# Two of four weight-block sums per seven-product unit: from VectorE to adding transfers

## The chip, the cores and the metric

One core of one Trainium2 chip runs the whole program. The metric is device time in microseconds (us), from the first to the last instruction of one execution and what lies around it; for the kernel before, the median of three timed executions is given. A separate execution was taken with the hardware profiler, and all rows below are from that one.

## The reference

One inference step of a two-layer decoder trunk in float32, for 512 prompt tokens and 8 x 8 sample tokens (576 columns in all), model width 1024:

```
x = x + 0.5 * ffn(x);  x = x + mixer(rmsnorm(x));  x = x + 0.5 * ffn(x)      # twice: S5 mixer, then gated-convolution mixer
ffn(x) = (silu(h @ Wgate) * (h @ Wup)) @ Wdown,  h = rmsnorm(x),  Wgate, Wup: 1024 x 4096,  Wdown: 4096 x 1024
```

At the end stand a final norm and the new states. The four FFN halves and the convolution mixer (whose input projection is 1024 x 3072) hold nearly all of the multiplications.

## The kernel before, in words

Each float32 product is made of three TensorE products on split operands: an operand is written as a high part (`h`, made by ScalarE's copy, ACT in the rows) and the remainder (`l`, made by VectorE's subtraction, DVE in the rows), and h·h, l·h and h·l are summed in PSUM. So every weight block has to be loaded, split by ACT and then by DVE before TensorE (PE) may use it.

The first FFN half, the S5 mixer and the first part of its output projection run in a fixed order. From line 1610 on (`later`), the rest runs from a list made by a planner: `late_glu`, `late_ffn(0, 1)`, `late_ffn(1, 0)`, `late_conv`, `late_ffn(1, 1)`. In this part the gate, up and convolution-input projections use a seven-product scheme (`class Seven`, line 1049): a unit of 1024 x 256 weights, one 1 MB transfer, is cut in four blocks, and with four sums of weight blocks and the matching sums of activations seven block products of 12 matmuls each (84 in all, 288 columns each) take the place of eight. There are 108 such units: 32 in each of the three FFN halves and 12 in the convolution. In an FFN half a group of four units is followed by a group of four "down" steps (192 matmuls, two 1 MB transfers, the plain three-product scheme of `Step` and `step_ops`).

`Seven.weights` (lines 1059 to 1084) prepares one unit from its loaded tile `raw` (seen as `v`, block (h, a) being `v[:, :, h, a]`):

- line 1066, `s1`: `st[1] = v(0,1) + v(1,1)`, on DVE;
- line 1070, `s3`: `v(0,1) = v(0,1) + v(0,0)` in place, on DVE, after `s1`, since it overwrites what `s1` reads;
- line 1080: `st[0] = st[1] + v(0,0)`, on DVE; line 1074, `s4`: `s4f = st[0] + v(1,0)`, on DVE;
- three splits of 128 x 1024 into `wh` (line 1044, ACT) and `wl` (line 1047, DVE): `r1` from `v(0,·)` after `s3`, `s12` from `st` after line 1080, `r2` from `v(1,·)` after the load; and a split of 128 x 512 (`s4h`, `s4l`) after `s4`.

What sets the order: `in_order` (line 938) replays a list of operations with modelled costs. Loads (SP queue), PE and GpSimd operations (POOL in the rows) keep the order in which they were created; for DVE and ACT the planner picks, among those that can begin first, the one with the earliest due time (`late`). The instruction streams come out in this order and each engine then runs its stream strictly in order, waiting on semaphores. Buffers are part of the plan: two `raw` tiles (a unit's tile is free when `r1`, `r2` and `s4` are done, and only then does the SP queue load the unit after the next into it), four pairs `wh`/`wl` (taken in the order r1, s12, r2 of unit after unit), two `st` tiles, two `s4f` tiles, four PSUM tiles.

Between two stages (an FFN half and the next one, or the convolution) DVE has other work that PE waits for: the residual additions (line 1346), the sums of squares (line 1236), the sums and remainders of the new activations (`tk`, lines 1175 to 1191), the norm (lines 1253 to 1264). Within the convolution it also has the gates and the three taps (lines 1487 to 1491). The seven products are evacuated by ACT (lines 1142, 1145, 1147, 1154) and DVE (1148, 1151, 1156).

Of the kernel before, what the change touches and what calls it, by code (L numbers as in the profile page):

```python
# [13 lines left out]
MUL, ADD, SUB = ALU.mult, ALU.add, ALU.subtract  # L14

P = 128
# [9 lines left out]
G = 64  # L26
# [7 lines left out]
def trunk_kernel(ctx: ExitStack, tc: tile.TileContext, a, o):  # L34
    nc = tc.nc
    V, S, T, GP, SP = nc.vector, nc.scalar, nc.tensor, nc.gpsimd, nc.sync
# [64 lines left out]
    class Unit:  # L101
        def __init__(self, src, nk, w):
            self.src, self.nk, self.w, self.left = src, nk, w, w * nk // D
# [807 lines left out]
            self.pool, self.n, self.t = pool, n, 0.0  # L911

    class Op:
        def __init__(self, eng, cost, fn, deps=(), take=(), give=(), due=12.0):
            self.eng, self.cost, self.fn, self.give = eng, cost, fn, give
            self.deps = [d for d in deps if d is not None]
            self.take, self.users, self.end = take, [], None
            self.left = len(self.deps)
            for d in self.deps:
                d.users.append(self)  # L920
            if eng == "PE":
                self.late = clock[0]
                clock[0] += cost
            else:
                self.late = clock[0] + due
            for p in take:
                fifo.setdefault(p, []).append(self)
            ops.append(self)
# [3 lines left out]
    def dve(n, fn, deps=(), **kw):  # L932
        return Op("V", 0.12 + 1.085e-3 * n, fn, deps, **kw)
# [4 lines left out]
    def in_order():  # L938
        for o in reversed(ops):
            for d in o.deps:  # L940
                d.late = min(d.late, o.late - d.cost)
        now = {e: 0.0 for e in ("PE", "V", "S", "SP", "G", "J")}
        queue = {e: [o for o in ops if o.eng == e] for e in ("PE", "SP", "G")}
        at = {e: 0 for e in queue}
        ready = {e: [o for o in ops if o.eng == e and not o.left] for e in ("V", "S", "J")}
        count = len(ops)

        def begin(o, t):
            for d in o.deps:
                t = max(t, d.end + 0.15)  # L950
            need = {}
            for p in o.take:
                need[p] = need.get(p, 0) + 1
            for p, n in need.items():
                if any(f is not o for f in fifo[p][:n]) or len(free[p]) < n:
                    return None
                t = max(t, sorted(free[p])[n - 1] + 0.15)
            return t

        while count:  # L960
            best = None
            for e, t in now.items():
                if e in queue:
                    c = queue[e][at[e]:at[e] + 1]
                    c = [o for o in c if not o.left]
                else:
                    c = ready[e]
                c = [(b, o) for b, o in ((begin(o, t), o) for o in c) if b is not None]
                if c:
                    first = min(b for b, _ in c)  # L970
                    b, o = min(((b, o) for b, o in c if b <= first + 0.1), key=lambda bo: bo[1].late)
                    if best is None or b < best[0]:
                        best = (b, o)
            assert best, [(e, queue[e][at[e]].fn) for e in queue if at[e] < len(queue[e])]
            b, o = best
            for p in o.take:
                fifo[p].remove(o)
                free[p].remove(min(free[p]))
            o.end = b + o.cost
            if o.eng != "J":  # L980
                o.fn()
                now[o.eng] = o.end
            if o.eng in queue:
                at[o.eng] += 1
            else:
                ready[o.eng].remove(o)
            for h in o.give:
                h.n -= 1
                h.t = max(h.t, o.end)
                if h.n == 0:  # L990
                    free[h.pool].append(h.t)
            for u in o.users:
                u.left -= 1
                if not u.left and u.eng in ready:
                    ready[u.eng].append(u)
            count -= 1
        return now
# [11 lines left out]
    def late_tile(pool, tag, shape, dt, name):  # L1009
        return B[pool].tile(list(shape), dt, name=nm(name), tag=tag)  # L1010
# [21 lines left out]
    def load_op(u):  # L1032

        if not hasattr(u, "load_op"):
            u.hold = Hold("raw", u.left)
            u.load_op = Op("SP", 5.0, u.load, take=["raw"])
        return u.load_op

    def split_ops(box, src, n, tags, deps, pool="w", give=()):

        def hi():
            p = B["s4"] if pool == "s4" else wp
            box["h"], box["l"] = (p.tile([P, 4, n, P], F32R, name=nm(t), tag=t) for t in tags)
            S.activation(box["h"], src(), AF.Copy)  # L1044

        h = scal(512 * n, hi, deps, take=[pool])
        return dve(512 * n, lambda: V.tensor_sub(box["l"], src(), raw32(box["h"])), [h], give=give)  # L1047

    class Seven:
# [9 lines left out]
        def weights(self):  # L1059
            u = self.unit  # L1060
            ld = load_op(u)

            def s1():
                v = self.v()
                self.st = late_tile("st", "st", [P, 4, 2, P], F32, "st")
                V.tensor_add(self.st[:, :, 1], v[:, :, 0, 1], v[:, :, 1, 1])

            def s3():
                v = self.v()
                V.tensor_add(v[:, :, 0, 1], v[:, :, 0, 1], v[:, :, 0, 0])  # L1070

            def s4():
                self.s4f = late_tile("s4f", "s4f", [P, 4, 1, P], F32, "s4f")
                V.tensor_add(self.s4f[:, :, 0], self.st[:, :, 0], self.v()[:, :, 1, 0])

            st = Hold("st", 2)
            a = dve(512, s1, [ld], take=["st"])
            b = dve(512, s3, [a])
            self.k_r1 = split_ops(self.r1, lambda: self.v()[:, :, 0], 2, ("wh", "wl"), [b], give=[u.hold])
            c = dve(512, lambda: V.tensor_add(self.st[:, :, 0], self.st[:, :, 1], self.v()[:, :, 0, 0]), [a])  # L1080
            self.k_s12 = split_ops(self.s12, lambda: self.st, 2, ("wh", "wl"), [c], give=[st])
            d = dve(512, s4, [c], take=["s4f"], give=[st, u.hold])
            self.k_r2 = split_ops(self.r2, lambda: self.v()[:, :, 1], 2, ("wh", "wl"), [ld], give=[u.hold])
            self.k_s4 = split_ops(self.s4, lambda: self.s4f, 1, ("s4h", "s4l"), [d], pool="s4", give=[Hold("s4f", 1)])
# [831 lines left out]
```

## Time and profile before

| What | Value |
|---|---|
| Three timed executions | 2775.16, 2779.84, 2782.81 us (median 2779.84) |
| Profiled execution, its time | 2784.35 us |
| Profiled execution, its span | 2782.6 us |
| PE, DVE, ACT, POOL busy share | 98%, 72%, 41%, 5% |
| Mean granted TensorE clock | 0.985 |
| DMA traffic | 285.07 MB, mean 102 GB/s |

The profiled execution lies 4.5 us (0.16%) above the median of the timed ones, and its own time 1.75 us above its span. PE's busy time comes from pipelined matmuls with modelled ends, so the count of matmuls in a stretch tells more than the share.

### The profile page before, as it was taken

What the parts mean: (1) busy time and instruction counts of PE and PEld (TensorE: products, weight loads), DVE (VectorE), ACT (ScalarE), POOL (GpSimd) and SP (SyncE); (2) the same over time, 40 slices, a digit from 0 to 9 for tenths busy, and PEclk for the clock granted to TensorE, in tenths of its full rate; (3) what the DMA queues carried; (4) which work ended last, traced back from release to release, by engine and by line L of the source; (5) the groups of instructions that cost most, each with busy time, mean ns of one, the idle gap of its engine ahead of it and who ended that gap; (6) DMA issues with size and microseconds to landing.
All of it is one profiled execution on the core that took longest, in us unless ns stands there. A gap on an engine that the chain in (4) does not pass through costs nothing.

```text
span 2782.6 us, 47469 instructions
## 1 busy us (share of the span) xinstructions
PE 2716.7 (98%) x20398; PEld 2691.4 (97%) x20398; DVE 2005.1 (72%) x2719; ACT 1148.6 (41%) x1638; POOL 134.7 (5%) x213
## 2 busy tenths in 40 slices
PE   8999999999999999999999999999899999999997
PEld 8999999998999999999989999999899999999997
DVE  5767655547558777777797777777898877777775
ACT  4222243423335444444464444434545544444444
POOL 3010122202200000000000000000000000000000
PEclk9999999998899999999999999999999999999999
DMA  6256444537322223332222332322222222333231
GB/s 134 87 157 167 136 132 131 155 121 248 117 81 77 91 92 91 92 92 92 92 62 92 92 92 92 92 91 92 66 87 92 77 91 92 92 92 92 91 92 50
DMA packets 227267, 285.07 MB, mean 102 GB/s; under 512 B 17460, under 2 KB 179616, under 8 KB 227024
## 3 DMA queue, kind: packets, MB, share of 16 engines
q1 hardware_dynamic: 217504, 256.86, 30.6%
q0 software_dynamic: 9376, 24.98, 3.0%
q8 instruction: 160, 2.62, 0.4%
q10 hardware_dynamic: 176, 0.20, 0.1%
q14 instruction: 51, 0.42, 0.0%
HBM read 260.19 MB, written 21.80 MB: 101 GB/s over the span
## 4 chain that ended last, share of the span: by engine, by line
PE 91%; DVE 6%; DMA 1%; ACT 1%; issue 1%; POOL 0%; POOLq 0%; DVEq 0%; ACTq 0%
PE ps L138 48%; PE ps L1110 40%; PE ps L1654 1%; DVE wl L1047 1%; DVE tk L1191 1%; PE ps L777 0%; DMA raw<-in_ffn_w_gate_up_dram 0%; PE ps L776 0%; DVE acc L1236 0%; PE ps L603 0%; DMA prow<-in_conv_w_dram 0%; DVE scr L764 0%; DVE g L756 0%; PE ps L1677 0%; DVE scr L765 0%
## 5 line engine op out<-in xcount | busy, mean ns | idle before, releaser
L1110 PE MATMUL ps<-tk,wh 128*128 128x288 f32 x5184 | 1061.3, 297 | 7.5 <-DVE tk L1191 2.9
L1110 PEld LDWEIGHTS ps<-tk,wh 128*128 128x128 f32 x5184 | 843.3, 189 | 11.3 <-DVE tk L1191 4.0
L1110 PE MATMUL ps<-tk,wl 128*128 128x288 f32 x2592 | 767.4, 296 | 8.3 <-DVE wl L1047 8.3
L138 PE MATMUL ps<-h,wh 128*128 128x288 f32 x3968 | 694.4, 295 | 0.1
L138 PEld LDWEIGHTS ps<-h,wh 128*128 128x128 f32 x3968 | 584.5, 188 | 1.9 <-DVE x L227 1.3
L1110 PEld LDWEIGHTS ps<-tk,wl 128*128 128x128 f32 x2592 | 490.2, 189 | 10.5 <-DVE wl L1047 10.0
L138 PE MATMUL ps<-h,wl 128*128 128x288 f32 x1984 | 424.0, 295 | 0.0
L138 PE MATMUL ps<-xg,wh 128*128 128x288 f32 x2048 | 362.9, 298 | 1.9 <-DVE xg L1850 1.9
L1044 ACT ACTIVATE wh<-raw 128x1024 fp32r<-128x1024 f32 x216 | 227.5, 1053 | 240.8 <-PE ps L138 231.3
L138 PEld LDWEIGHTS ps<-h,wl 128*128 128x128 f32 x1984 | 319.6, 188 | 0.0
L1047 DVE TENSOR_TENSOR wl<-raw,wh 128x1024 fp32r<-128x1024 f32 x216 | 263.6, 1220 | 67.5 <-ACT wh L1044 67.4
L138 PEld LDWEIGHTS ps<-xg,wh 128*128 128x128 f32 x2048 | 304.1, 190 | 4.5 <-DVE xg L1850 2.2
L1346 DVE SCALAR_TENSOR_TENSOR x<-ps,x 128x576 f32<-128x576 f32 x184 | 139.1, 757 | 130.1 <-PE ps L138 128.1
L138 PE MATMUL ps<-xg,wl 128*128 128x288 f32 x1024 | 220.0, 297 | 0.0
L1110 PE MATMUL ps<-tk,s4h 128*128 128x288 f32 x864 | 193.0, 299 | 10.4 <-DVE c L1148 7.4
L1044 ACT ACTIVATE wh<-st 128x1024 fp32r<-128x1024 f32 x108 | 114.5, 1060 | 196.6 <-PE ps L138 115.7
L127 DVE TENSOR_TENSOR wl<-raw,wh 128x1024 fp32r<-128x1024 f32 x103 | 126.7, 1231 | 85.4 <-ACT wh L126 85.2
L1322 ACT ACTIVATE wh<-raw 128x1024 fp32r<-128x1024 f32 x113 | 119.4, 1056 | 151.1 <-PE ps L138 121.1
L1325 DVE TENSOR_TENSOR wl<-raw,wh 128x1024 fp32r<-128x1024 f32 x113 | 137.8, 1220 | 46.7 <-ACT wh L1322 46.6
L138 PEld LDWEIGHTS ps<-xg,wl 128*128 128x128 f32 x1024 | 165.9, 190 | 0.0
L126 ACT ACTIVATE wh<-raw 128x1024 fp32r<-128x1024 f32 x103 | 108.4, 1053 | 126.1 <-PE ps L138 76.2
L1110 PEld LDWEIGHTS ps<-tk,s4h 128*128 128x128 f32 x864 | 146.1, 190 | 13.1 <-issue 7.0
(367 smaller groups left out, 3187.8 us busy)
## 6 DMA issues: line engine op xcount, KB each, us to landing
raw<-in_ffn_w_gate_up_dram SPq DMA_DIRECT2D x126, 1024.0 KB, 5.9
raw<-in_ffn_w_down_dram SPq DMA_DIRECT2D x64, 1024.0 KB, 5.1
raw<-in_conv_w_in_dram SPq DMA_DIRECT2D x12, 1024.0 KB, 5.1
raw<-in_ssm_w_glu_dram SPq DMA_DIRECT2D x8, 1024.0 KB, 5.3
pri<-pw_d SPq DMA_DIRECT2D x16, 256.0 KB, 9.3
bri<-bb_d SPq DMA_DIRECT2D x16, 256.0 KB, 8.5
ws_d<-ws POOLq DMA_DIRECT2D x8, 512.0 KB, 4.8
wy_d<-wy POOLq DMA_DIRECT2D x8, 512.0 KB, 2.9
```

The source lines that it names most:

```text
L126: S.activation(self.wh, src, AF.Copy)
L127: V.tensor_sub(self.wl, src, raw32(self.wh))
L138: T.matmul(self.ps[m][:, b, :NH], wt[:, k, c], x[:, part, b * NH:(b + 1) * NH], start=k == 0 and wt is self.wh and part == 0, stop=k == se ...
L1044: S.activation(box["h"], src(), AF.Copy)
L1047: return dve(512 * n, lambda: V.tensor_sub(box["l"], src(), raw32(box["h"])), [h], give=give)
L1110: T.matmul(ps, wt[:, k, sel], box[k][:, part, slot], start=term in ("Q1", "Q2", "S3") and k == 0 and wt is w["h"] and part == 0, stop=k == ...
L1191: V.tensor_sub(got[j][:, 1, a:b], s, raw32(got[j][:, 0, a:b]))
L1322: S.activation(st.wh, u.v[:, :, st.sub * w:(st.sub + 1) * w], AF.Copy)
L1325: st.ready = dve(D, lambda: V.tensor_sub(st.wl, u.v[:, :, st.sub * w:(st.sub + 1) * w], raw32(st.wh)), [h], give=[u.hold])
L1346: stt(h2(x[:, i]), ps()[:, :, :NH], scale, h2(x[:, i]), op0=MUL, op1=ADD)
L1654: T.matmul(pst[i][:, 0, :NH], wt[:, k, m * P:(m + 1) * P], hs[k][:, part, cols], start=k == 0 and wt is st.wh and part == 0, stop=k == 3 a ...
```

## The change

In `weights`, the sums of lines 1066 and 1070 no longer run on VectorE. For `st[1]`, the SP queue copies block (0,1) from the weights in DRAM into `st` once more, and a transfer issued by GpSimd then adds block (1,1) from DRAM onto it. For `v(0,1)`, a transfer issued by GpSimd adds block (0,0) from DRAM onto the loaded tile. So each unit has three more transfers of 256 KB, one on the SP queue and two on GpSimd's. The sums of lines 1080 and 1074 stay on VectorE. The planner's operations get a `lag`: time until the result can be used, in which the queue is already free.

```
     class Op:
-        def __init__(self, eng, cost, fn, deps=(), take=(), give=(), due=12.0):
+        def __init__(self, eng, cost, fn, deps=(), take=(), give=(), due=12.0, lag=0.0):
...
-                d.late = min(d.late, o.late - d.cost)
+                d.late = min(d.late, o.late - d.cost - d.lag)
...
-            o.end = b + o.cost
+            o.end = b + o.cost + o.lag
...
-                now[o.eng] = o.end
+                now[o.eng] = b + o.cost
...
-            u.load_op = Op("SP", 5.0, u.load, take=["raw"])
+            u.load_op = Op("SP", 4.5, u.load, take=["raw"], lag=1.0)
...
-            def s1():
-                v = self.v()
+            def block(h, m):
+                return u.src.rearrange("(k h p) (m c) -> p k h m c", h=2, p=P, m=2)[:, :, h, m]
+
+            def a21():
                 self.st = late_tile("st", "st", [P, 4, 2, P], F32, "st")
-                V.tensor_add(self.st[:, :, 1], v[:, :, 0, 1], v[:, :, 1, 1])
-
-            def s3():
-                v = self.v()
-                V.tensor_add(v[:, :, 0, 1], v[:, :, 0, 1], v[:, :, 0, 0])
+                SP.dma_start(self.st[:, :, 1], block(0, 1))
...
-            a = dve(512, s1, [ld], take=["st"])
-            b = dve(512, s3, [a])
+            b = Op("G", 0.7, lambda: GP.dma_start(self.v()[:, :, 0, 1], block(0, 0), accum_op=ADD), [ld], lag=4.0)
+            a = Op("SP", 1.3, a21, take=["st"], lag=2.0)
+            a = Op("G", 0.7, lambda: GP.dma_start(self.st[:, :, 1], block(1, 1), accum_op=ADD), [a], lag=4.0)
```

The split `r1` now depends on `b` (the adding transfer onto `v(0,1)`), and line 1080's sum depends on the second `a` (the adding transfer onto `st`).

## Rows read from the trace of the kernel before

**Rows 1.** Page: busy time of the engines; then shares of the chain of waits.

```profile
PE 2716.7 (98%) x20398; PEld 2691.4 (97%) x20398; DVE 2005.1 (72%) x2719; ACT 1148.6 (41%) x1638; POOL 134.7 (5%) x213
PE 91%; DVE 6%; DMA 1%; ACT 1%; issue 1%; POOL 0%; POOLq 0%; DVEq 0%; ACTq 0%
```

**Rows 2.** Busy by stretch: length, PE, PEld, DVE, ACT, POOL (x count), PEclk, DMA share, GB/s.

```profile
831.00:864.00 33.00, 28.30 (x184) 26.23 (x183) 26.38 (x36) 18.73 (x28) 0.00 (x0) 0.95 0.13 36
864.00:1372.00 508.00, 508.00 (x3827) 507.96 (x3825) 377.62 (x463) 215.04 (x295) 0.00 (x0) 1.00 0.30 92
...
1402.00:1440.00 38.00, 31.07 (x198) 29.50 (x198) 34.29 (x47) 20.87 (x30) 1.04 (x2) 0.91 0.22 63
...
1979.00:2040.00 61.00, 53.88 (x360) 51.75 (x359) 54.20 (x73) 29.86 (x51) 0.00 (x0) 0.92 0.22 70
2040.00:2150.00 110.00, 104.48 (x765) 102.67 (x764) 100.42 (x138) 52.46 (x99) 0.00 (x0) 0.98 0.29 94
...
2188.00:2218.00 30.00, 26.57 (x187) 24.98 (x186) 24.99 (x34) 17.94 (x26) 0.00 (x0) 1.00 0.18 55
```

**Rows 3.** Groups by line and shape: the two sums in question, whole run.

```profile
L1066 DVE TENSOR_TENSOR st<-raw 128x512 f32<-128x512 f32 x108 | 74.5, 689 | 76.7 <-DMA raw<-in_ffn_w_gate_up_dram 76.2
L1070 DVE TENSOR_TENSOR raw<-raw 128x512 f32<-128x512 f32 x108 | 73.8, 683 | 0.1
```

**Rows 4.** Timeline of VectorE and TensorE: start, length, line, count, [idle before <- releaser].

```profile
832.13 0.69 DVE L1066 TENSOR_TENSOR st<-raw 128x512 f32<-128x512 f32 x1
839.72 0.53 PE L1110 MATMUL ps<-tk,wh 128*128 128x288 f32 x2 [1.12 <-DVE tk L1191]
...
851.03 0.69 DVE L1066 TENSOR_TENSOR st<-raw 128x512 f32<-128x512 f32 x1 [0.40 <-DMA raw<-in_ffn_w_gate_up_dram]
855.02 0.61 PE L1110 MATMUL ps<-tk,s4l 128*128 128x288 f32 x1 [1.28 <-DVE s4l L1047]
...
1407.76 0.42 PE L1110 MATMUL ps<-tk,wl 128*128 128x288 f32 x1 [2.33 <-DVE wl L1047]
1430.38 0.37 PE L1110 MATMUL ps<-tk,s4h 128*128 128x288 f32 x1 [3.29 <-DVE c L1148]
...
2069.28 0.40 PE L1110 MATMUL ps<-tk,wl 128*128 128x288 f32 x1 [1.10 <-DVE wl L1047]
2104.98 0.40 PE L1110 MATMUL ps<-tk,wl 128*128 128x288 f32 x1 [1.78 <-DVE wl L1047]
```

**Rows 5.** Chain of waits in order of time: start, us, what.

```profile
1209.68 44.53 PE ps L1110 x336
...
1405.97 0.60 DVE raw L1070
...
2064.38 0.53 DVE raw L1070
...
2101.05 0.60 DVE raw L1070
```

**Rows 6.** Timeline of SP, VectorE and ScalarE: a unit within an FFN, then one in the convolution.

```profile
1223.84 0.37 SPq L111 DMA_DIRECT2D raw<-in_ffn_w_gate_up_dram  x1
1229.85 0.69 DVE L1066 TENSOR_TENSOR st<-raw 128x512 f32<-128x512 f32 x1 [0.26 <-DMA raw<-in_ffn_w_gate_up_dram]
1235.47 1.05 ACT L1044 ACTIVATE wh<-raw 128x1024 fp32r<-128x1024 f32 x1
...
2084.03 0.69 DVE L1066 TENSOR_TENSOR st<-raw 128x512 f32<-128x512 f32 x1
2087.41 1.05 ACT L1044 ACTIVATE wh<-raw 128x1024 fp32r<-128x1024 f32 x1
```

**Rows 7.** Transfers issued by GpSimd: issue time (ns min/median/max); then KB each, us to landing.

```profile
L444 POOL DMA_DIRECT2D b_in<-in_ssm_b_re_dram x1: 1729/1729/1729, 39.3 to 39.3; - x1
...
b_in<-in_ssm_b_re_dram POOLq DMA_DIRECT2D x1, 256.0 KB, 6.2
y<-y_d POOLq DMA_DIRECT2D x8, 288.0 KB, 3.5
```

More of the change, by code (lines that the diff above doesn't have):

```diff
@@ L913, in trunk_kernel @@
     class Op:
-        def __init__(self, eng, cost, fn, deps=(), take=(), give=(), due=12.0):
-            self.eng, self.cost, self.fn, self.give = eng, cost, fn, give
+        def __init__(self, eng, cost, fn, deps=(), take=(), give=(), due=12.0, lag=0.0):
+            self.eng, self.cost, self.fn, self.give, self.lag = eng, cost, fn, give, lag
             self.deps = [d for d in deps if d is not None]
```

## Prediction

> **What bounds the kernel now.** I read the page's busy shares first: PE is busy 98%, DVE 72%, POOL 5% [rows 1]. As PE's ends are modelled, the busy share alone doesn't say that PE is the limit, so I turned to the chain of waits, 91% of which is PE and 6% DVE [rows 1]: the change takes work from an engine that holds a sixteenth of the chain. Then the busy time by stretch. From 864 to 1372 us, an FFN half in the planned part, PE issues 3827 matmuls in 508.00 us with no gap: 0.1327 us each, at the full granted clock [rows 2]. DVE is idle a quarter of that time. No relief of DVE can shorten such a stretch, and the other two planned FFN halves repeat it. Against that pace the stretches between the stages lose time: length less count x 0.1327 gives 8.6 us in 831 to 864, 11.7 in 1402 to 1440, 13.2 in 1979 to 2040, 8.5 in 2040 to 2150 (the convolution) and 5.2 in 2188 to 2218 [rows 2], 47 us in all. There DVE is busy 80 to 91% of the time, and twice PE's granted clock falls to a mean of 0.91 or 0.92. These 47 us are the ceiling of what the change can give. The timeline then shows which DVE instruction ends PE's waits there [rows 4], and the chain of waits whether a removed sum stands in front of it [rows 5].
>
> **What it removes.** Two of DVE's sums in each of 108 units: 74.5 + 73.8 = 148 us of DVE's 2005 [rows 1, 3]. In the FFN halves that is worth nothing (PE covers it; if PE were quicker, it would come to count). Stage by stage, against the profiled execution:
>
> - GLU to FFN, 831 to 864. The sum of line 1066 at 832.13 stands in DVE's stream ahead of the `tk` for which PE waits 1.12 us at 839.72: 0.6 us (its 0.69, less the overlap of neighbours that the chain shows as pieces of 0.60 [rows 5]). A second one at 851.03 first waits 0.40 us for its load and then runs ahead of the `s4l` for which PE waits 1.28 us at 855.02 [rows 4]: 0.4 + 0.6 = 1.0. Together -1.6. Convolution to FFN (2188 to 2218) has the same order: -1.5.
> - FFN to FFN, 1402 to 1440. Line 1070's sum at 1405.97 is a piece of the chain, 0.60 us [rows 5], right before the remainder for which PE waits 2.33 us at 1407.76 [rows 4]: -0.6. Between the two DVE works for the new activations. What is late next is PE's wait of 3.29 us at 1430.38 for line 1148 [rows 4], which stands behind the norm; no removed sum is in that stretch of the chain, so it only moves forward. FFN to convolution repeats it: -0.6.
> - Convolution. PE waits 1.10 us at 2069.28 and 1.78 at 2104.98 for remainders of `r1` [rows 4], each with a sum of line 1070 in front in the chain (0.53 and 0.60) [rows 5] and line 1066's beside it. DVE is busy 100.42 of 110 us there and loses about 1.2 us of work in each unit [rows 2, 5], so I count both waits as gone: -2.9.
>
> Removed: 1.6 + 1.5 + 0.6 + 0.6 + 2.9 = 7.2 us.
>
> **What it adds.** On SP 108 issues of about 0.37 us [rows 6], 40 us in all on a queue that has nothing else to do between loads. The copy into `st` stands in front of the next unit's load and waits for an `st` tile; that tile is given back with `s12` and `s4`, before the `raw` tile for which the load waits anyway, so it holds nothing up: 0. On POOL 216 issues; the dearest row of the nearest kind, 256 KB in small pieces, has 1.73 us [rows 7], so at most 3.5 us in each unit's 11.13 us (44.53 / 4 [rows 5]). POOL has no work of its own in the FFN stretches (0.00 busy [rows 2]); behind the waiting adding transfers are only the next unit's, some outputs, and one cache load well ahead of its use: 0. Traffic grows by 108 x 3 x 262,144 bytes = 85 MB on 285; at a DMA share of 0.30 in the FFN halves [rows 2], half as much again is 0.45, with the read of the target perhaps 0.6: not a bound.
>
> The cost that the trace does not show is the time until an adding transfer has landed, since no transfer of this kind is in it. It lies in the path of `r1` in place of DVE's two sums. Bounds: from 3.5 us (288 KB, plain, by POOL) to 12.4, twice the 6.2 us of `b_in` (256 KB from DRAM, by POOL), as each piece reads two operands [rows 7]. I take 6.2: same size, same issuer, same direction; its pieces are finer (16 floats, by the reference's layout, against 128 here), which makes up for part of the second read.
>
> Is it covered? The load issued at 1223.84 has landed by 1229.85, 6.0 us later; ACT's split of that unit's `r1` starts at 1235.47 [rows 6], held back by the `wh` tiles, not by data: 5.6 us of cover. The group of four units starts at 1209.68, so this fourth one starts at 1209.68 + 3 x 11.13 = 1243.07 [rows 5]. With 1.05 us for ACT's copy and at most 1.4 for DVE's remainder (twice 0.69 [rows 3]), `r1` may land 1243.07 - 2.45 - 1229.85 = 10.8 us after the load before PE waits. At 6.2 the FFN halves pay 0. In the convolution, where no down steps give time, a unit is landed by 2084.03 and split at 2087.41 [rows 6]: 3.4 us of cover. Landing 6.2 later would make that split 2.8 us late. Between 0 and 2.8 for such a unit; I take 1 us in all, because part of it falls into the time between the split and its first matmul, and other convolution units wait for DVE, not for data.
>
> **Sum.** -7.2 + 1.0 = -6.2 us on the profiled 2784.35, that is 2778.2; the profiled execution stands 4.5 us above the median 2779.84, so for the median 2773.6, -0.22%. A measurement here can tell about 0.3% (8.3 us) from no change; the forecast is a gain just too small for that.
>
> **Rivals.**
> 1. *The adding transfers land late (slower).* Place: `r1`'s split on ACT and line 1080 on DVE, both in strictly ordered streams, so the evacuations behind them are held too. Price: at 12.4 us PE waits 1.6 us for the fourth unit of each group, 24 groups in three halves, 38 us, and the convolution adds something up to 6.2 us a unit. With the 6.2 us of the sum, 2779.8 + 38 - 6.2 = 2812 or more. It decides from about 10.8 us on; below that only the convolution pays. For it: two accumulates of a unit follow each other on one queue, and ACT and DVE stop for them. Against it: 5 us between the 6.2 of the nearest row and the point. The Trainium skill's page "Collectives: The Full Stack", section "The bandwidth ceiling: the fold count and why AG ≠ RS ≠ AR", says that a reducing transfer moves half as much as a copy because each chunk is read from two sources. No run here shows that yet; by that rule the upper bound, 12.4, would be the likelier one and the sum would be this rival's.
> 2. *DVE's relief reaches further.* If the planner, with DVE free earlier, puts line 1148 in front of other work, the two waits of 3.29 us go as well: -6.2 - 6.6 = -12.8, 2767. For it: it is a matter of order only. Against it: the due times of those instructions don't change.
> 3. *The change does not do what it says on the path.* The sums go, but the planner fills the same slots, now waiting for transfers, and PE's waits stay: 2780.
>
> **How the numbers follow.** Forecast 0.52, its own range 2767 to 2779: the terms are fixed sums of rows, but the new plan shifts every order by a little; of it 0.21 lies under 2771.5 (0.3%) and 0.31 above. Rival 1 0.25, rival 2 0.15, rival 3 0.08. So faster 0.21 + 0.15 = 0.36, same 0.31 + 0.08 = 0.39, slower 0.25. The range reaches from 2763, below rival 2, to 2800, which takes in landings a little past the deciding point and leaves out the far end of rival 1, about 0.15 of it with 0.04 below.
>
> **What would show it.** Right: the groups of lines 1066 and 1070 are gone and DVE's busy time is near 1857 us; the FFN stretches stay at 0.1327 us a matmul with the granted clock at 1.00; the waits at 855, 2069 and 2105 are gone, that at 1407 is 0.6 shorter, that of 3.29 remains; the adding transfers land in 5 to 8 us. Rival 1 would show as waits of ACT's line 1044 and DVE's line 1080 for `raw` and `st` transfers and gaps of PE before `r1`'s matmuls within the FFN groups. Wrong altogether: a lower clock or longer matmuls in the FFN stretches, or the 1 MB loads landing much later than 6 us beside the new traffic.

## The result and the profile after

The changed kernel is slower: median 2796.12 us (four executions, 2791.82 to 2798.94) against 2780.24 for the kernel before on the same chip (2775.16 to 2782.81), ratio 1.0058 with an interval of 1.0038 to 1.0078. Forecast was 2773.6, so a small gain was expected and 16 us were lost. The profiled execution took 2794.82 us, with a span of 2793.0. That is 10.4 us more than the profiled span before, and not 16, mostly because the profiled execution of before was itself 4.5 us slower than its median.

The page of the kernel after, busy time and the chain of waits by engine, answering [rows 1]:

```profile
PE 2715.9 (97%) x20398; PEld 2685.3 (96%) x20398; DVE 1874.2 (67%) x2503; ACT 1151.0 (41%) x1638; POOL 415.3 (15%) x429
...
PE 85%; DVE 7%; DMA 5%; issue 2%; ACT 1%; POOL 0%; SPq 0%; POOLq 0%; DVEq 0%; ACTq 0%
```

VectorE is relieved by 131 us, and yet the share of DMA in the chain has risen from 1 to 5%. What follows cuts both kernels at the same work: from the first seven-product matmul of a stage to the first matmul of the plain scheme behind it (GLU to FFN, FFN to FFN, FFN to convolution with the convolution, convolution to FFN). Busy time in these four stretches of the kernel before, columns as in [rows 2]:

```profile
830.40:903.41 73.01, 68.31 (x486) 66.25 (x485) 60.14 (x77) 42.98 (x60) 0.00 (x0) 0.98 0.25 78
1402.74:1478.89 76.15, 69.22 (x486) 67.65 (x485) 67.29 (x86) 43.39 (x61) 1.04 (x2) 0.96 0.28 85
1979.01:2133.43 154.42, 142.24 (x1015) 138.69 (x1013) 139.82 (x191) 74.56 (x136) 0.00 (x0) 0.97 0.28 89
2187.74:2257.38 69.64, 66.21 (x486) 64.62 (x485) 58.81 (x75) 41.83 (x58) 0.00 (x0) 1.00 0.27 85
```

and of the kernel after:

```profile
828.36:901.39 73.03, 67.84 (x487) 64.85 (x485) 55.20 (x69) 42.75 (x60) 10.36 (x8) 1.00 0.55 124
1402.95:1479.83 76.88, 68.26 (x487) 66.04 (x486) 65.30 (x83) 44.90 (x63) 10.61 (x8) 0.98 0.55 124
1979.62:2142.05 162.43, 144.78 (x1014) 139.50 (x1012) 128.89 (x172) 73.83 (x137) 26.04 (x20) 0.97 0.60 133
2196.35:2266.49 70.14, 66.89 (x487) 64.79 (x486) 56.23 (x70) 41.89 (x59) 10.35 (x8) 1.00 0.60 136
```

The convolution takes 8.0 us more (162.43 for 154.42) although VectorE has 11 us less to do in it; the other three are 0.0, 0.7 and 0.5 longer. The FFN groups between add 2.2 us (first half) and 1.3 (last half, to the end of the run). Why the convolution is longer, the chain of waits within it shows (start, us, what):

```profile
2046.60 8.30 DMA raw<-in_conv_w_in_dram
2054.93 1.06 ACT wh L1044
...
2087.88 8.03 DMA raw<-in_conv_w_in_dram
```

These two pieces begin where GpSimd issues the adding transfer onto `raw` and end with its landing; ACT's split of `r1` follows at once. What sets these two apart, the SP queue shows: it issues the next unit's 1 MB load 0.59 and 0.68 us behind them.

```profile
2047.19 0.37 SPq L111 DMA_DIRECT2D raw<-in_conv_w_in_dram  x1
2088.56 0.37 SPq L111 DMA_DIRECT2D raw<-in_conv_w_in_dram  x1
```

The other eight adding transfers onto `raw` in this stretch have the next load 4.6 us or more behind them and land after 4.3 to 5.4 us. All ten, least, median and most:

```profile
DMA to landing us min/median/max: 4.3/4.8/8.3
```

PE's timeline has the waits for the two late splits at 2056.04 to 2057.30 and 2097.04 to 2098.30, and at 2076.30 and 2117.28 what is left of the waits at 2069 and 2105 of before [rows 4]:

```profile
2056.04 0.40 PE L1109 MATMUL ps<-tk,wh 128*128 128x288 f32 x1 [1.46 <-ACT wh L1044]
2057.30 0.40 PE L1109 MATMUL ps<-tk,wl 128*128 128x288 f32 x1 [0.86 <-DVE wl L1047]
2076.30 0.40 PE L1109 MATMUL ps<-tk,wl 128*128 128x288 f32 x1 [0.86 <-DVE wl L1047]
...
2097.04 0.40 PE L1109 MATMUL ps<-tk,wh 128*128 128x288 f32 x1 [1.99 <-ACT wh L1044]
...
2117.28 0.40 PE L1109 MATMUL ps<-tk,wl 128*128 128x288 f32 x1 [0.86 <-DVE wl L1047]
```

Each of the two late landings costs twice. Around them the busy times, columns as in [rows 2], are:

```profile
2050.00:2057.30 7.30, 4.99 (x37) 4.54 (x35) 3.09 (x4) 1.60 (x3) 1.94 (x2) 1.00 1.22 223
2057.30:2070.00 12.70, 12.67 (x82) 12.43 (x83) 10.62 (x15) 5.61 (x15) 0.63 (x1) 0.87 0.44 92
2090.00:2098.30 8.30, 5.45 (x40) 5.00 (x39) 3.39 (x4) 1.77 (x3) 2.56 (x2) 1.00 1.08 218
2098.30:2110.00 11.70, 11.67 (x74) 11.43 (x75) 9.84 (x14) 5.60 (x15) 1.30 (x1) 0.85 0.48 77
```

First PE waits: 37 and 40 matmuls in these lengths are 2.4 and 3.0 us short of the pace of 0.1327 us a matmul. Then, with PE busy again, the granted clock has a mean of 0.87 and 0.85: part of the stretch runs at the lower of its two levels, 1.2 in place of 2.4 GHz, and another 1.8 and 1.9 us are lost. Together that is about 9.1 us, an estimate from these rows.

In the FFN halves it is the other transfer that is late. Groups by line and shape of the kernel after, line 1079 being line 1080 of before:

```profile
L1077 POOL DMA_DIRECT2D st<-in_ffn_w_gate_up_dram x96 | 166.8, 1737 | 3.7 <-DMA st<-in_ffn_w_gate_up_dram 3.0 <-issue 0.7
L1075 POOL DMA_DIRECT2D raw<-in_ffn_w_gate_up_dram x96 | 123.7, 1288 | 1417.2 <-DMA raw<-in_ffn_w_gate_up_dram 892.6 <-DVE c L1150 100.6 <-DVE s4f L1072 69.4
L1079 DVE TENSOR_TENSOR st<-st,raw 128x512 f32<-128x512 f32 x108 | 74.5, 690 | 171.5 <-DMA st<-in_ffn_w_gate_up_dram 171.3
```

VectorE stands 171.3 us in all in front of line 1079, with everything that comes behind it in its stream. Mostly PE has enough work meanwhile; once in the first FFN half it has not (timeline, VectorE, then TensorE):

```profile
1028.79 0.69 DVE L1079 TENSOR_TENSOR st<-st,raw 128x512 f32<-128x512 f32 x1 [1.97 <-DMA st<-in_ffn_w_gate_up_dram]
...
1035.13 0.44 DVE L1147 SCALAR_TENSOR_TENSOR c<-c,ps 128x288 f32<-128x288 f32 x1
...
1035.63 0.41 PE L1109 MATMUL ps<-tk,s4h 128*128 128x288 f32 x1 [1.47 <-DVE c L1147]
```

### The profile page after: what moved, and what is told of

It reads as the page before. It is cut to its first block, busy times and chain, and to the rows that moved or that the text cites. A ratio compares the mean times of both kernels' runs of the same rounds, so it can differ in the third digit from the quotient of the medians.

```text
span 2793.0 us, 48164 instructions
## 1 busy us (share of the span) xinstructions
PE 2715.9 (97%) x20398; PEld 2685.3 (96%) x20398; DVE 1874.2 (67%) x2503; ACT 1151.0 (41%) x1638; POOL 415.3 (15%) x429
## 3 DMA queue, kind: packets, MB, share of 16 engines
q0 software_dynamic: 123424, 81.62, 19.7%
## 4 chain that ended last, share of the span: by engine, by line
PE 85%; DVE 7%; DMA 5%; issue 2%; ACT 1%; POOL 0%; SPq 0%; POOLq 0%; DVEq 0%; ACTq 0%
PE ps L138 45%; PE ps L1109 37%; DMA st<-in_ffn_w_gate_up_dram 2%; DMA raw<-in_conv_w_in_dram 1%; DVE wl L1047 1%; DMA raw<-in_ffn_w_gate_up_dram 1%; PE ps L1653 1%; DVE tk L1190 1%; PE ps L777 1%; PE ps L776 1%; PE ps L1800 0%; DVE c L1276 0%; DMA xin<-in_x_prompt_dram 0%; DVE acc L1235 0%; PE ps L728 0%
## 5 line engine op out<-in xcount | busy, mean ns | idle before, releaser
L1109 PEld LDWEIGHTS ps<-tk,wh 128*128 128x128 f32 x5184 | 843.1, 189 | 25.4 <-DVE tk L1190 8.5
L1044 ACT ACTIVATE wh<-raw 128x1024 fp32r<-128x1024 f32 x216 | 227.5, 1054 | 268.1 <-PE ps L138 226.5
L1075 POOL DMA_DIRECT2D raw<-in_ffn_w_gate_up_dram x96 | 123.7, 1288 | 1417.2 <-DMA raw<-in_ffn_w_gate_up_dram 892.6
L1079 DVE TENSOR_TENSOR st<-st,raw 128x512 f32<-128x512 f32 x108 | 74.5, 690 | 171.5 <-DMA st<-in_ffn_w_gate_up_dram 171.3
L1321 ACT ACTIVATE wh<-raw 128x1024 fp32r<-128x1024 f32 x113 | 119.3, 1056 | 152.5 <-PE ps L138 121.1
L1077 POOL DMA_DIRECT2D st<-in_ffn_w_gate_up_dram x96 | 166.8, 1737 | 3.7 <-DMA st<-in_ffn_w_gate_up_dram 3.0
```

Source lines behind the costliest of these rows:

```text
L1075: b = Op("G", 0.7, lambda: GP.dma_start(self.v()[:, :, 0, 1], block(0, 0), accum_op=ADD), [ld], lag=4.0)
L1077: a = Op("G", 0.7, lambda: GP.dma_start(self.st[:, :, 1], block(1, 1), accum_op=ADD), [a], lag=4.0)
L1109: T.matmul(ps, wt[:, k, sel], box[k][:, part, slot], start=term in ("Q1", "Q2", "S3") and k == 0 and wt is w["h"] and part == 0, stop=k == ...
L1321: S.activation(st.wh, u.v[:, :, st.sub * w:(st.sub + 1) * w], AF.Copy)
```

## The experiments

Ratios are to the kernel before, run on the same chip beside each. "Convolution" is the stretch of 154.42 us above, from one profiled execution of each run; e12, which moves no sum, differs from before by 0.9 us there, so a difference of about 1 us says nothing.

| Run | Ratio (interval) | Convolution, us |
|---|---|---|
| changed kernel | 1.0058 (1.0038 to 1.0078) | 162.4 |
| e1 FFN units only | 1.0021 (1.0006 to 1.0036) | 154.9 |
| e2 convolution units only | 1.0026 (1.0015 to 1.0038) | 160.5 |
| e3 st alone | 1.0035 (1.0021 to 1.0048) | 157.5 |
| e4 no adding transfers | 0.9976 (0.9968 to 0.9985) | 149.9 |
| e5 raw alone | 1.0010 (1.0001 to 1.0018) | 153.6 |
| e6 measured times in the plan | 1.0051 (1.0039 to 1.0063) | 161.0 |
| e7 st first in both queues | 1.0065 (1.0053 to 1.0077) | 157.6 |
| e8 first two units of a stage | 1.0025 (1.0013 to 1.0036) | 157.3 |
| e9 order kept, none issued | 0.9966 (0.9954 to 0.9978) | 148.8 |
| e10 order kept, st's issued | 0.9973 (0.9963 to 0.9982) | 150.3 |
| e11 order kept, raw's issued | 0.9989 (0.9980 to 0.9997) | 155.8 |
| e12 the planner's times alone | 1.0012 (1.0003 to 1.0022) | 153.5 |
| e13 order kept, plain copies | 0.9973 (0.9963 to 0.9983) | 149.5 |
| e14 st's second by SP, plain | 1.0011 (1.0002 to 1.0020) | 159.9 |
| e15 st alone, measured times | 1.0048 (1.0036 to 1.0060) | 159.4 |
| e16 st alone, load as before | 1.0036 (1.0025 to 1.0048) | 155.1 |
| e17 both sums on GpSimd | 1.0157 (1.0143 to 1.0171) | 160.1 |
| e18 line 1070's sum on GpSimd | 1.0010 (1.0001 to 1.0019) | 151.7 |

### Where it is lost: e1 and e2

```diff
+            if self.adds:        # e1: ypair is not None; e2: ypair is None
                 (the three transfers)
+            else:
+                a = dve(512, s1, [ld], take=["st"])
+                b = dve(512, s3, [a])
```

> Transfers only in the 96 FFN units; the 12 convolution units make their sums on VectorE as before. Theory (in the convolution the split of r1 waits for the adding transfer onto raw, 7.7 to 8.3 us in the chain, and that is where most is lost, about 9 of the 10.4 us between the two profiled spans): the convolution has its old length again, the span is 2782 to 2787 us, ratio to before 1.000 to 1.002. Rival (the loss comes from the added traffic or from the FFN units, which are 96 of 108): 2790 us or more, ratio 1.004 or more.

> Transfers only in the 12 convolution units; the 96 FFN units make their sums on VectorE as before. Theory (the convolution alone loses about 9 us): span 2788 to 2794 us, ratio to before 1.002 to 1.005, with PE's waits for wh and wl of r1 in the convolution as in the changed kernel. Rival (the loss is in the FFN units and the stage changes): 2779 to 2784 us, ratio 0.999 to 1.001.

The convolution is as expected in both: 154.9 without transfers in it, 160.5 with. But 12 of 108 units do not carry the whole loss. The two ratios are 0.21 and 0.26% above one, 0.58 with both, and e1's lies just above what the theory gave it. The FFN units have a share. How large it is, e1 says only roughly: its twelve executions lie between 2774.89 and 2797.89 us, and the profiled one, with 2796.32, is the second slowest.

### Landing or order: e4, e9, e10, e11

First the two adding transfers were taken out of the plan as well:

```diff
-            b = Op("G", 0.7, lambda: GP.dma_start(..., accum_op=ADD), [ld], lag=4.0)
+            b = ld
-            a = Op("G", 0.7, lambda: GP.dma_start(..., accum_op=ADD), [a], lag=4.0)
```

> Leaves out both adding transfers: st[1] holds block (0,1) alone and v(0,1) is not added to. The copy into st and VectorE's relief stay. Theory (the landing of the adding transfers costs, the relief itself is worth what the prediction summed, 7 us): ratio to before 0.996 to 0.999, and the convolution shorter than before's. Rival (the relief is worth nothing, or the new order of the plan or the copy's issue ahead of the loads costs): ratio 1.000 to 1.005.

0.9976: the relief is there. But the plan made another order of it. So next the entries stayed in the planner's list, and only the issue was left out, of both (e9), of `raw`'s (e10) or of `st`'s (e11); every other instruction keeps its place:

```diff
-            b = Op("G", 0.7, lambda: GP.dma_start(..., accum_op=ADD), [ld], lag=4.0)
+            b = Op("G", 0.7, lambda: None, [ld], lag=4.0)       # e9, e10
-            a = Op("G", 0.7, lambda: GP.dma_start(..., accum_op=ADD), [a], lag=4.0)
+            a = Op("G", 0.7, lambda: None, [a], lag=4.0)        # e9, e11
```

> The changed kernel with both adding transfers left out (not issued), but with their entries still in the planner's list, so that every engine has the same instructions in the same order as in the changed kernel. Leaves out two of the four sums. Theory (the landings of the adding transfers are what costs): the ratio to before falls from 1.006 to 0.996 to 1.000, no transfer of raw or st is left in the chain of the convolution, whose stretch falls from 162.4 us to 150 to 155. Rival (the order of VectorE and ScalarE that the planner made is what costs, as the run with st alone hints, whose chain in the convolution has no transfer in it): the ratio stays at 1.002 or more and the convolution at 157 us or more.

> The same, with only the adding transfer onto raw left out (its entry stays in the planner's list, the order of all engines is the changed kernel's). Theory (r1's landing costs): the convolution falls from 162.4 to under 157 us and the ratio to 1.000 to 1.003. Rival (st's chain costs): convolution 159 us or more, ratio 1.004 or more.

> The same, with only the adding transfer onto st left out. Theory (r1's landing costs in the convolution, st's only in the FFN halves and stage changes): the convolution stays at 159 us or more, VectorE's wait at line 1079 falls from 171 us to under 15, ratio 1.002 to 1.005. Rival (st's chain costs): convolution under 157 us, ratio 1.000 to 1.002.

The four stretches of e9:

```profile
829.15:898.98 69.83, 66.60 (x487) 64.74 (x486) 55.52 (x69) 43.16 (x60) 0.00 (x0) 1.00 0.32 97
1397.98:1472.34 74.36, 69.23 (x486) 67.70 (x485) 62.98 (x79) 43.91 (x62) 1.03 (x2) 0.95 0.34 101
1972.13:2120.93 148.80, 139.69 (x1015) 136.41 (x1013) 128.46 (x172) 74.02 (x137) 0.00 (x0) 0.99 0.35 110
2175.23:2243.74 68.51, 66.21 (x486) 64.62 (x485) 54.43 (x67) 42.00 (x58) 0.00 (x0) 1.00 0.33 102
```

With the same order and no landing to wait for, every one is shorter than before: by 3.2, 1.8, 5.6 and 1.1 us. The ratio is 0.34% under one, so the order by itself is not what costs. The adding transfers, issue and landing, cost 1.0058 - 0.9966 = 0.92% (give or take 0.23, from the two intervals), some 25.6 us; between the two profiled spans it is 2793.0 - 2767.6 = 25.4, of which 162.43 - 148.80 = 13.6 in the convolution. Alone, `raw`'s transfer costs 0.9989 - 0.9966 = 0.23% (convolution 155.85, 7.0 us more than e9's), `st`'s 0.07%, which the intervals don't tell from nothing (150.33). Neither expectation of e10 and e11 foresaw that: `raw`'s transfer is the dearer one, but leaving out either ends most of the loss, and the pair costs three times the sum. In the convolution of e11 one late landing of the kind above is left: issued at 2073.74 with the next load 0.51 us behind it, `raw`'s transfer lands after 8.07 us, and no adding transfer onto `st` is issued in this run. e10's rows for `st`'s transfer show what the neighbour on GpSimd's queue does (group, then landing):

```profile
L1077 POOL DMA_DIRECT2D st<-in_ffn_w_gate_up_dram x96 | 123.4, 1286 | 1535.0 <-DMA st<-in_ffn_w_gate_up_dram 700.8 <-DVE x L1345 476.8 <-DVE c L1150 179.5
...
st<-in_ffn_w_gate_up_dram POOLq DMA_DIRECT2D x96, 256.0 KB, 4.6
```

Alone it is issued in 1286 ns and lands after 4.6 us in the median; behind `raw`'s it takes 1737 ns and 5.9 us, and starts later.

### Is it the adding: e13 and e14

```diff
-  GP.dma_start(self.v()[:, :, 0, 1], block(0, 0), accum_op=ADD)
+  GP.dma_start(self.v()[:, :, 0, 1], block(0, 0))          # e13 only
-  GP.dma_start(self.st[:, :, 1], block(1, 1), accum_op=ADD)
+  GP.dma_start(self.st[:, :, 1], block(1, 1))              # e13; e14: SP.dma_start
```

> The changed kernel with both of GpSimd's transfers issued as plain copies in place of adding ones: same size, same targets, same waits, same order of all engines. Two of the four sums are not made. Theory (a transfer of this size by GpSimd costs its issue and landing, whether it adds or not): the landings stay at 4.3 to 4.8 us (raw) and 5.3 to 6.0 (st) and the ratio at 1.004 to 1.008. Rival (the adding is dear, since the target is read as well): the landings fall by 1 us or more each and the ratio to 1.002 or less.

> The changed kernel with st's second transfer issued by the SP queue, as a plain copy (st[1] then holds block (1,1) alone), in place of GpSimd's adding transfer; raw's adding transfer stays on GpSimd. Theory (the pair costs 0.92% where each alone costs 0.07 and 0.23%, because st's transfer stands behind raw's on one queue): ratio falls to 0.998 to 1.002, VectorE's wait at line 1079 to under 90 us. Rival (two landings in a unit are late together whatever the queue, or SP's wait for the first copy holds loads back): ratio 1.004 or more.

In e13 `v(0,1)` and `st[1]` hold a single block each in place of a sum; targets, sizes and order are the changed kernel's. The theory on it fell, and plainly. Its groups, the same three lines as above:

```profile
L1079 DVE TENSOR_TENSOR st<-st,raw 128x512 f32<-128x512 f32 x108 | 73.9, 684 | 9.2 <-DMA st<-in_ffn_w_gate_up_dram 8.8
L1075 POOL DMA_DIRECT2D raw<-in_ffn_w_gate_up_dram x96 | 72.1, 751 | 1493.4 <-DMA raw<-in_ffn_w_gate_up_dram 868.3 <-DVE c L1155 281.5 <-DVE s4f L1072 72.4
L1077 POOL DMA_DIRECT2D st<-in_ffn_w_gate_up_dram x96 | 72.0, 750 | 14.0 <-DMA st<-in_ffn_w_gate_up_dram 6.6 <-issue 5.0
```

Its DMA queue of GpSimd (packets, MB, share of 16 engines' span) and landings (KB, median us):

```profile
q0 software_dynamic: 26656, 81.62, 10.3%
...
raw<-in_ffn_w_gate_up_dram POOLq DMA_DIRECT2D x96, 256.0 KB, 3.3
st<-in_ffn_w_gate_up_dram POOLq DMA_DIRECT2D x96, 256.0 KB, 3.5
```

The same of the kernel after:

```profile
q0 software_dynamic: 123424, 81.62, 19.7%
...
raw<-in_ffn_w_gate_up_dram POOLq DMA_DIRECT2D x96, 256.0 KB, 4.7
st<-in_ffn_w_gate_up_dram POOLq DMA_DIRECT2D x96, 256.0 KB, 5.9
```

and of e9, where neither is issued:

```profile
q0 software_dynamic: 9376, 24.98, 2.9%
```

For the same bytes an adding transfer of 256 KB took (123424 - 9376) / 216 = 528 packets, a copy 80. Of all 16 DMA engines it took (19.7 - 2.9)% x 2793.0 / 216 = 2.17 us against (10.3 - 2.9)% x 2767.0 / 216 = 0.95, 2.3 times as much; it was issued in 1.29 to 1.74 us against 0.75 and landed 1.4 and 2.4 us later. With copies in the same places the ratio is 0.9973: of the 0.92% only 0.07, which the intervals don't tell from nothing, goes with two more transfers as such, and the rest with their adding.

In the convolution a load, a copy and two adding transfers come close together. The DMA engines' busy tenths from 2040 to 2060 us, half a microsecond each, kernel after:

```profile
DMA  0005599999992000446999999999999999993799
```

The like window of e13, 2027.7 to 2047.7 us, and the landings of its copies onto `raw` in the convolution (least, median, most):

```profile
DMA  0004589999992000878999999999100096991000
...
DMA to landing us min/median/max: 3.4/3.5/5.2
```

The engines are full for 17 slices, 8.5 us at a stretch, with the adding transfers, 4.5 with copies. And a load right behind does not delay a copy: in e13 two have the next load 0.59 and 0.99 us behind them, and land after 3.6 and 3.5 us where the adding ones took 8.3 and 8.0. e14 stands between, at 1.0011, with VectorE's wait at line 1079 down to 8.9 us: within what the theory gave (its convolution, though, is still 159.9 us: one adding transfer there has the next load 0.52 us behind it and lands after 8.2); but two things were changed in it (queue and adding), so it doesn't tell them apart. Two adding transfers on two queues were not tried; how the extra cost of the pair splits into queue and DMA load stays open.

### The planner's times: e6, e7, e12

```diff
 e6: b: 1.3, lag=5.7    a21: 1.3, lag=5.0    a: 1.3, lag=5.0
 e7: a21 ahead of the load on SP, a ahead of b on GpSimd
 e12: the sums as before; only Op("SP", 4.5, u.load, ..., lag=1.0)
```

> The changed kernel with the planner's times for the transfers set to what the trace shows: adding transfer onto raw 1.3 + 5.7 in place of 0.7 + 4.0, copy into st 1.3 + 5.0 in place of 1.3 + 2.0, adding transfer onto st 1.3 + 5.0 in place of 0.7 + 4.0. Theory (the landings themselves are on the path in the convolution, and no order of VectorE can hide them): VectorE's wait at line 1079 falls from 171 us to under 90, but the convolution stays 4 to 8 us longer than before and the ratio at 1.003 to 1.006. Rival (the loss is VectorE and ScalarE standing in an order that was planned with landings that are too short): the ratio falls to 0.998 to 1.002 and the convolution to within 2 us of before.

> The changed kernel with st's copy ahead of the unit's load on SP and st's adding transfer ahead of raw's on GpSimd. Theory A (st's chain of two transfers behind the load is what VectorE stands for): the wait at line 1079 falls below 100 us and the ratio to 1.001 to 1.004. Theory B (r1's landing is what costs): ratio unchanged, 1.005 to 1.007. Against both: if the copy's wait for an st tile holds back the load behind it, 1.007 or more.

> The kernel before with one part of the change alone: the planner's field for a lag and the load at 4.5 + 1.0 in place of 5.0. No transfer is added, no sum is moved. Theory: worth nothing, ratio 0.999 to 1.001. Rival (a change of the planner's times alone reorders VectorE and ScalarE at the stage changes and costs): 1.0015 to 1.004, and the runs with transfers in a part of the units owe a part of their loss to it.

e6 bears the theory out: told the true times, the planner cuts VectorE's wait at line 1079 from 171 to 22 us, and the kernel is as slow as before that (1.0051). So taking away VectorE's standing did not by itself help. The late splits of `r1` are still there, in part in another place: from FFN to FFN it takes 84.4 us (76.88 in the changed kernel), PE waiting 4.32 and 3.92 us for line 1044. In e7 the convolution gains 4.8 us and the rest loses more: line 1079 now waits 139 us for the load itself, whose landing rose from 6.1 to 6.6 us behind the copy. e12 costs 0.12% without any transfer: the theory's band ended at 0.10, so a small part of every run that keeps the new load time (all but e16) may be owed to it; its interval, from 0.03 to 0.22%, reaches into the band.

### Other shares of the work: e3, e5, e8, e15 to e18

e3 keeps `st`'s transfers and makes line 1070's sum on VectorE (`b = dve(512, s3, [ld])`); e15 and e16 are e3 with other planner times; e5 keeps `raw`'s transfer behind VectorE's sum of line 1066; e8 has all transfers, but only in the first two units of each stage (`s.adds = len(sevens) < 2`).

> Only st[1] is made by transfers (copy by SP, adding transfer by GpSimd); v(0,1) is summed on VectorE right after the load, with no order against st[1] any more. Theory (the wait of r1's split for the adding transfer onto raw is what costs): the convolution's chain has no adding transfer onto raw, its length is within 2 us of before's, ratio to before 0.998 to 1.002. Rival (VectorE standing at line 1079 for st, 171 us in the changed kernel, is what costs): that wait stays at 120 us or more, and the ratio stays at 1.004 or more.

> The mirror of the run with st alone: only the adding transfer onto raw is left, st[1] is summed on VectorE (and the transfer waits for that sum, which reads the block it overwrites). Theory (in the convolution the split of r1 comes one landing, 7 to 8 us, after the load): the stretch of the convolution, 154.4 us before and 162.4 in the changed kernel, is 4 to 8 us longer than before, ratio to before 1.002 to 1.005. Rival (what costs is st's chain of copy and adding transfer): the convolution within 1.5 us of before, ratio 0.999 to 1.001.

> Transfers only in the first two units of each FFN half and of the convolution, whose weights are loaded before the stage begins, with the planner's times as measured; all other units make their sums on VectorE. Theory (the relief is worth something where the landing is covered by an early load, and costs elsewhere): ratio to before 0.9975 to 0.9995, with the stretches of the stage changes 1 to 3 us shorter. Rival (the transfers cost wherever they are, or the relief is worth nothing without the other units): 1.000 to 1.003.

> The run with st alone by transfers (line 1070's sum on VectorE), with the planner's times for the two transfers as measured (1.3 + 5.0 and 1.3 + 4.5). Theory (there the loss was an order of VectorE, its chain in the convolution has no transfer; the landing of st alone is worth 2 us): with other times the order changes and the ratio is 0.997 to 1.001. Rival (an honest plan makes VectorE's order no better): 1.002 or more.

> The run with st alone by transfers, with the load's time in the planner as before (5.0, no lag). Theory as for the run with measured lags: an order that is drawn anew, ratio 0.997 to 1.002. Rival (st's transfers cost 0.3% in any order): 1.002 to 1.005.

Most of these expectations missed. In e5 the convolution is 0.8 us shorter than before, not 4 to 8 longer, although `raw`'s transfer is in its path. Its landings there are shorter: the first has a load 0.16 us behind it and lands after 6.9 us, the others have none within 2.7 us and land after 4.4 to 4.8. The loss in the convolution thus goes with the landings of 8 us, and not with every adding transfer in the path; no run moves the load alone, so this is read from rows and not tested. e8 costs 0.25% with transfers in 8 units: in its profile FFN to FFN takes 80.9 us with PE's granted clock at a mean of 0.92 (76.15 and 0.96 before). And `st` alone costs 0.35 to 0.48% in three different orders, though its landing was worth 0.07% in e10. In e3 no transfer stands in the convolution's chain; the chain has VectorE's work in line (start, us, what):

```profile
2072.40 1.27 DVE c L1280
2073.67 1.15 DVE wl L1047
...
2074.86 24.00 PE ps L1113 x179
```

That pointed to the order, but two new draws (e15, e16) were no better. Why one sum back on VectorE costs more than both is open.

If a late sum is the trouble, a short one on GpSimd itself should do, without a transfer: e17 makes both there, e18 line 1070's alone.

```diff
+            a = Op("G", 1.4, s1, [ld], take=["st"])      # GP.tensor_add; e18: on VectorE as before
+            b = Op("G", 1.4, s3, [a])                    # GP.tensor_add
```

> Both sums of lines 1066 and 1070 are made by GpSimd's own additions (no transfer at all), with the load at 4.5 + 1.0 in the planner. The nearest row, a sum of 128x576 on GpSimd, has 1.41 to 1.51 us, so about 1.3 us for 128x512, where the adding transfer took 1.29 to issue and 4.7 to land. Theory (VectorE's relief is worth the 0.34% that the run with the order kept shows, and only the late landings ate it): r1 comes 2.6 us after the load in place of 1.4, ratio 0.996 to 0.999. Rival (relief of VectorE pays only where nothing stands between load and split, or VectorE gets slower beside GpSimd): 1.000 to 1.004.

> Only the sum of line 1070 on GpSimd, after VectorE's sum of line 1066; no transfer is added. Theory: half of VectorE's relief, r1 1.3 us after VectorE's sum, ratio 0.998 to 1.000. Rival (two engines in turn between load and split cost more than the relief is worth): 1.001 to 1.004, as the run with raw alone by a transfer had 1.001.

e18 came out where its rival began (1.0010), and e17 is the slowest of all. Its timeline in an FFN group, VectorE and GpSimd (L1073 and L1077 are the two moved sums, L1087 the sum of line 1080):

```profile
1238.11 1.30 POOL L1073 TENSOR_TENSOR st<-raw 128x512 f32<-128x512 f32 x1 [9.85 <-DMA raw<-in_ffn_w_gate_up_dram]
1238.20 2.29 DVE L1047 TENSOR_TENSOR wl<-st,wh 128x1024 fp32r<-128x1024 f32 x1
1239.49 2.16 POOL L1077 TENSOR_TENSOR raw<-raw 128x512 f32<-128x512 f32 x1
1240.42 1.78 DVE L1087 TENSOR_TENSOR st<-st,raw 128x512 f32<-128x512 f32 x1
```

While GpSimd adds, VectorE's subtraction of 1.22 us takes 2.29 and its sum of 0.69 takes 1.78; VectorE's busy time is back at 2024.1 us. None of the versions with all four sums beat the kernel before.

## Why the prediction was wrong

**What was removed: right in size, and not for its reasons alone.** For the four stretches the steps gave 1.6, 0.6, 3.5 (0.6 + 2.9) and 1.5 us, in all 7.2; without landings (e9) they lose 3.2, 1.8, 5.6 and 1.1, in all 11.7, and the ratio of 0.9966 makes 9.4 us. The convolution's two waits were forecast to go; they shrank from 1.10 and 1.78 to 0.86 each, in e9 too. What came in their place is partly the clock, which no step had priced: its mean in the rows is 0.98 and 0.97 before and 1.00 and 0.99 in e9 for the first and the third stretch, and 0.96 and 0.95 for the second, in all about 4 us, an estimate from rounded means. That the total fits is in part luck. A part of rival 2 came with it: PE's wait of 3.29 us for line 1148 [rows 4] is 2.15 in the kernel after (line 1147):

```profile
1409.77 0.61 PE L1109 MATMUL ps<-tk,wl 128*128 128x288 f32 x1 [1.93 <-DVE wl L1047]
...
1431.21 0.37 PE L1109 MATMUL ps<-tk,s4h 128*128 128x288 f32 x1 [2.15 <-DVE c L1147]
```

The first row answers to the wait of 2.33 us at 1407.76, forecast to be 0.6 shorter: 0.4.

**The step that failed: "I take 1 us in all" for the late `r1` in the convolution, and nothing for the FFN halves.** In its place the runs show 25.6 us for the adding transfers, 13.6 of them in the convolution; e11 has 7.0 us there for this transfer alone. Two things were wrong in the step. The landing: 6.2 us was taken, which lies above the medians of 4.7 and 5.9, but the two landings in the path took 8.3 and 8.0, each with the next load issued right behind. The cover: the same paragraph had found 3.4 us of it for a convolution unit and a split 2.8 us late, and then let most of that go. PE waited 2.3 us (1.46 + 0.86) and 2.9 (1.99 + 0.86) behind the two, and the lower clock that followed cost 1.8 and 1.9 more, for which the step had no term.

**A missing step: cover was worked out for `r1` only.** `st` has two transfers in a row, a copy behind the load (median 6.6 us) and an adding one behind that (5.9), with GpSimd's two issues in line. No due time of line 1080's sum was set against this chain; rival 1 named the line, but its deciding point of 10.8 us was counted for `raw`. It shows as 171 us of VectorE's standing and as the gap of PE in an FFN group above. What that cost is not settled: in e6 the standing was nearly gone and the time was not better. The 0.62% that come only with both transfers (0.92 - 0.23 - 0.07, give or take 0.27 from the four intervals) are not split between this chain, the issue in line and the fuller DMA engines.

**POOL's issues at 0, traffic "not a bound".** The share of DMA was estimated at 0.45 to 0.6 in the mean, and the stretches above show 0.55 to 0.60. A mean hides the burst: for 8.5 us on end the engines were full, and an adding transfer in such a burst landed after 8.3 us. And issue on GpSimd was costed for its length only, not as the time by which the second transfer starts later.

**Rival 1 was the right one**, in kind and in its signs (ACT's line 1044 and VectorE's line 1080 waiting, gaps within the FFN groups), not in its place: it was priced in the FFN halves, 38 us, and against e9 they lost 2.6 us (first), nothing (second) and 2.7 (last, to the end of the run), where the convolution lost 13.6 and the three other stretches 7.4. By its deciding point it should not have come about at all. The Trainium skill's page "Collectives: The Full Stack", section "The bandwidth ceiling: the fold count and why AG ≠ RS ≠ AR", has a reducing transfer at half the rate of a copy, for its two reads; the 2.17 and 0.95 us of DMA time above, 2.3 times, agree with it in the main. The median landing, 4.7 against 3.3, grew less than that. Whether the second read or the 528 packets in place of 80 make the difference, no run tells.

**FFN stretches at 0** held for the second half (499.8 us against 500.1 from its first plain matmul to the convolution) and nearly for the others. The granted clock there had a mean of 1.00, as forecast. VectorE's busy time came to 1874 us where 1857 was forecast; it is 1880 in e9 too, so the landings don't make that difference, and what does is open.

## What to carry to other kernels

Before a sum goes from an engine to a transfer, write down for every consumer when its input lands and when the next engine in line wants it, chains of two transfers included, and in the stage with the least cover, not in the longest one. Take the landing from a place where the same neighbours are on the DMA engines: 4.7 us in the median was 8 with a load right behind. An engine that is a sixteenth of the chain may be relieved by 131 us of work, and inputs that land a few us late then cost more than that was worth. To find out whether an order or a landing costs, keep the order and leave the transfer out: here this one run parted +0.58% into -0.34 and +0.92.

## What was not expected of the hardware

- An adding transfer of 256 KB took 528 packets and 2.17 us of all 16 DMA engines, a plain one into the same place 80 packets and 0.95 us; GpSimd needed 1.29 us to issue the one, 0.75 for the other.
- A second adding transfer right behind a first took 5.9 us to land in the median, alone 4.6.
- With the next 1 MB load issued 0.5 to 0.7 us behind it, an adding transfer of 256 KB landed after 8.0 to 8.3 us (kernel after, e11 and e14), else mostly after 4.3 to 5.4; a plain copy with a load 0.6 us behind it landed after 3.6 (e13).
- GpSimd's additions beside VectorE slowed both: 128x512 took 1.28 us on GpSimd at the least and 1.80 in the median for the second sum, and VectorE's 1.22 us became 2.29. The Trainium skill's page "GPSIMD Engine Reference", section "1. Specifications", says that the two share their way to the on-chip memory and collide when VectorE reads two inputs; the rows of e17 agree.
